# A hybrid transformer layer on one core: the SBUF tiles laid out anew, weight units at the top, streaming operands from the bottom up

## Chip, cores and metric

The kernel runs on one core of a Trainium2 chip. The metric is the device time of one execution in microseconds (us); lower is better. The on-chip memory SBUF has 128 partitions, and a tile occupies the same range of bytes in each of them; all sizes and places below are bytes of one partition. TensorE (PE in the profile) multiplies a stationary operand, which is loaded first (LDWEIGHTS, PEld in the profile), with a moving one that streams through. VectorE is DVE, ScalarE is ACT, GpSimd is POOL, and SP issues most of the DMAs.

## The reference

One layer over 1024 latent tokens of width 1024 with a context of 256 tokens. The input is normed and modulated, one combined projection feeds three token mixers, each mixer's output is lifted to the full width, gated and summed, and an output projection adds to the stream. Then a gated MLP with a depthwise convolution of width 3 follows, and a final norm.

```python
h = x * rsqrt(mean(x*x)) * gain * (1 + scale) + shift          # adaLN, also for the context
q, k, v (A), q, k, v (B), q, f, b, i, g (C), gates = split(h @ w_in)
yA = sliding_window_attention(A)        # 8 heads of 64, 2 kv heads, window 128, sink, context keys
yB = global_attention(B)                # q and k normed, axial rotary
yC = bidirectional_recurrence(C)        # 4 heads of 128
merged = sum(sigmoid(gate_n) * (y_n @ w_branch_n) for n in (A, B, C))
x = x + m2 * (merged @ w_out)
h = adaLN(x)
u = depthwise_conv3(h @ w_up)           # 2 x 2816 columns
x = x + m5 * ((u[:2816] * silu(u[2816:])) @ w_down)
out = rms_norm(x)
```

## The kernel before

Every float32 operand is split into two parts of 12 bits, a high one and the rest (hh and hl, yh and yl, h2h and h2l, ah and al, ph and pl, KH and KL, wh and wl), and each product is three matmuls in the type fp32r: wh with the high part, wh with the low part, wl with the high part (lines 158, 159 and 160 of `gemm_cm`). There the weights are stationary, 128x128, and the other operand streams, 512 columns in one matmul. `gemm_tm` (lines 168 to 170) has them the other way round: the activations are stationary, and 256 columns of weights stream. In the profile's names the streaming operand of a matmul stands first behind the arrow and the stationary one second.

A weight unit (`w_unit`) is loaded by SP into `wr` (three buffers of 4 KB), ScalarE casts it to `wh` and VectorE subtracts to get `wl`. These three tags lie in the pool `wp`, 36,864 bytes, open for the whole kernel.

The stages, in the order in which they run:

- modulation and norm of context and latent stream; context projections (czf, czb, czv, ckv); the layer input in two parts, hh and hl (32 KB each, pool `hp`, closed as `hpool` after the attention);
- branch C, the recurrence: its projections are zq, zf, zb, zv, zg, five groups of 192 matmuls that stream hh and hl; between them the scores on small tiles;
- projections of A and B by tokens (tm), results to DRAM; `gate_unit` (gz) computes gate values to DRAM, and many of its units are kept as filler for the attention;
- attention A, then B, one call of `attention` each with a pool of its own, `at0` and `at1`. A call first loads and casts K and V of all tokens (KH, KL, VHL) and then goes through 16 iterations, two for each block of 128 queries. `weave` runs three generators by turns: the scores of the next iteration (sbl and others, which stream KH and KL), the values of this one, and gate units. `values` transposes a block of probabilities (pp), ScalarE and VectorE split it into ph and pl (`PV_BUF` = 3 buffers each), and po, streaming ph and pl with VHL stationary, adds it up. At the end of an iteration yT goes to DRAM (`y_d`);
- merge (`merge_up`, pool `mp`): for each branch in the order C, A, B four tiles of y come back from DRAM (two buffers) and are split into yh and yl (six buffers each); br are the products with `w_branch`. The sums go into xm, in two parts into h2h and h2l (32 KB each);
- output projection (wo), streaming h2h and h2l, then the norm, which writes the layer's second input into the same h2h and h2l;
- FFN: 44 column tiles of w_up, each for two halves of 512 tokens (up, 24 matmuls for each half), whose results are convolved, gated and split into ah and al (five buffers each), and in seven groups w_down (dn, streaming ah and al; dl for the last group), summed into xm. Then the final norm and the store.

Pools are stacked from the two ends of a partition: `side="right"` stacks from the top (229,344) down, the default from the bottom up. The constants end at 19,584. A pool that closes leaves its bytes to the next one; with `reuse_waits="tile"` a new tile waits for the last readers of those old tiles that lay on its bytes. So the place of a tile sets whom its first writer waits for. Within an engine's queue the order is that of the program as the scheduler arranged it, and a waiting instruction holds back those behind it.

Of the kernel before, what the change touches and what calls it, by code (L numbers as in the profile page):

```python
# [10 lines left out]
F32R = mybir.dt.float32r  # L11
# [4 lines left out]
PSUM = bass.MemoryType.PSUM  # L16
DRAM = bass.MemoryType.DRAM

P = 128
D = 1024  # L20
# [24 lines left out]
# channel tiles whose shift and scale the vector engine sums, and the tiles after which they are finished  # L45
# [3 lines left out]
# tiles whose squares are summed by GpSimd before the final norm  # L49
# [11 lines left out]
# heads whose softmax sums are finished together  # L61
NB = 1

# channel-major column tiles of the packed input projection
# [7 lines left out]
def build(tc, ins, out, dbg=None):  # L72
    nc = tc.nc
    V, A, G, T, SP = nc.vector, nc.scalar, nc.gpsimd, nc.tensor, nc.sync
    with ExitStack() as top:
        const = top.enter_context(tc.tile_pool(name="const", bufs=1))
        wp = top.enter_context(tc.tile_pool(name="wp", bufs=3))
# [22 lines left out]
        # the table of the sigmoid is loaded while c is under way  # L100
# [33 lines left out]
        def w_unit(src, nk, ncol, lo_eng=None):  # L134
            """one weight unit [128, nk, ncol] -> (hi, lo) in 12-bit parts"""
            cnt[0] += 1
            n = nk * ncol
            with tc.high_priority(offset=wprio[0]):
                raw = wp.tile([P, 1024], F32, tag="wr", name=f"wr{cnt[0]}", bufs=WR)
                SP.dma_start(raw[:, :n], src)  # L140
                hi = wp.tile([P, 1024], F32R, tag="wh", name=f"wh{cnt[0]}", bufs=WH)
                lo = wp.tile([P, 1024], F32R, tag="wl", name=f"wl{cnt[0]}", bufs=WL)
                A.copy(hi[:, :n], raw[:, :n])  # L143
                (lo_eng or V).tensor_tensor(out=lo[:, :n], in0=raw[:, :n], in1=hi[:, :n].bitcast(F32),  # L144
                                            op=ALU.subtract)
            return (hi[:, :n].rearrange("p (k n) -> p k n", k=nk),
                    lo[:, :n].rearrange("p (k n) -> p k n", k=nk))

        def gemm_cm(psl, w, h, cols, k0=0, c0=0, nk=None, first=True, last=True, order=None):
            """psl[128 out, tokens] (+)= w[:, k, c0:c0+128]^T h[:, k0+k, cols]; three passes"""  # L150
            wh, wl = w
            hh, hl = h
            nk = nk or wh.shape[1]
            c = slice(c0, c0 + P)
            for n, k in enumerate(order or range(nk)):
                s = first and n == 0
                e = last and n == nk - 1
                T.matmul(psl, wh[:, k, c], hh[:, k0 + k, cols], start=s, stop=False)  # L158
                T.matmul(psl, wh[:, k, c], hl[:, k0 + k, cols], start=False, stop=False)  # L159
                T.matmul(psl, wl[:, k, c], hh[:, k0 + k, cols], start=False, stop=e)  # L160

        def gemm_tm(psl, ws, h, toks, k0=0, nk=KT):
            """psl[128 tokens, cols] = sum_k h[:, k, toks]^T w[k]"""
            hh, hl = h
            for k in range(nk):
                wh, wl = ws[k // 4]
                s, e = k == 0, k == nk - 1
                T.matmul(psl, hh[:, k, toks], wh[:, k % 4, :], start=s, stop=False)  # L168
                T.matmul(psl, hh[:, k, toks], wl[:, k % 4, :], start=False, stop=False)  # L169
                T.matmul(psl, hl[:, k, toks], wh[:, k % 4, :], start=False, stop=e)  # L170

# [1 line left out]
        def rms_row(pool, parts, n, name, tag="b", on_pe=False):  # L173
            """1/sqrt(sum/D + eps) of the tokens, on every partition: PSUM [128, n]; parts: squares to be summed"""
# [7 lines left out]
            if on_pe:  # L182
                # the parts are summed as they are transposed
# [26 lines left out]
        def finish_h(t, r, a, bi, ohh, ohl, x=None):  # L210
            """x * a * r + bi in two parts; t, or x where it is given, is the scratch for x * a * r"""
            V.scalar_tensor_tensor(out=t, in0=t if x is None else x, scalar=a, in1=r, op0=ALU.mult, op1=ALU.mult)
            A.activation(ohh, t, AF.Identity, bias=bi)
            V.scalar_tensor_tensor(out=ohl, in0=t, scalar=bi, in1=ohh.bitcast(F32), op0=ALU.add, op1=ALU.subtract)  # L214

        with ExitStack() as s0:
# [9 lines left out]
            # shift and scale of both streams, one channel tile after the other  # L226
# [6 lines left out]
            def mod_done(i, pm):  # L233
                """shift and scale of channel tile i, and the tile of h"""
# [67 lines left out]
            # lower bounds: softmax over the (length one) layer axis, cumulative sum minus the first  # L302
# [19 lines left out]
            def lat_norm():  # L322
                # squares summed on two engines: tiles 0-3 and 4-7
# [52 lines left out]
            def ctx_kv():  # L376
                # attention keys and values of the context
# [25 lines left out]
            # suffix (forward) and prefix (backward) decay products over the 256 context tokens  # L403
# [28 lines left out]
        def gate_unit(pool, n, i, mode):  # L432
            """gate pre-activations of branch n, channel tile i -> dram"""
# [22 lines left out]
        def mod_rest(pool):  # L456
            """modulation chunks 2..5 of the latent stream"""
# [37 lines left out]
        with ExitStack() as sp3:  # L495
# [3 lines left out]
            # tables [t, tt, (C|S), 64]: A as they are, B with the head-norm gains  # L499
# [52 lines left out]
        n0 = 10 + GATES_A  # L552
        for br, units in ((0, gates[10:n0]), (1, gates[n0:])):
            with ExitStack() as sa:
                ap_ = sa.enter_context(tc.tile_pool(name=f"at{br}", bufs=2, side="right", reuse_waits="tile"))
                nf = 16 * len(units)
                gen = gate_units(ap_, units, "b")
                attention(tc, nc, ap_, br, ins, kv_d[br], q_d[br], y_d, mm2, bank, ident, identr, gen, nf)
# [5 lines left out]
        fp = top.enter_context(tc.tile_pool(name="fp", bufs=1, side="right", reuse_waits="tile"))  # L564
        xm = fp.tile([P, KT, L], F32, tag="xm", name="xm")
        f2 = top.enter_context(tc.tile_pool(name="f2", bufs=1, side="right", reuse_waits="tile"))
# [5 lines left out]
        f3 = ExitStack()  # L572
        ff = f3.enter_context(tc.tile_pool(name="ff", bufs=2, reuse_waits="tile"))
# [3 lines left out]
        def sumsq(parts, src, i, name, n, NPOOL):  # L577
            """squares of tile i, summed over the tiles by two engines; the last one stays apart"""
# [10 lines left out]
        # x_mix = x + m2 * (merged @ w_out), its norm; by token halves  # L589
# [21 lines left out]
        def up(f):  # L611
# [19 lines left out]
            ah = ff.tile([P, 1, L], F32R, tag="ah", name=f"ah{f}", bufs=5)  # L631
            al = ff.tile([P, 1, L], F32R, tag="al", name=f"al{f}", bufs=5)
# [11 lines left out]
        for g, ng in enumerate(FFN_GROUPS):  # L644
# [3 lines left out]
            if g < NG - 1:  # L648
                for i in range(KT):
                    if g == NG - 2 and i == KT // 2:  # L650
                        # the last tile of the hidden layer, with sums still to run behind it
# [8 lines left out]
            else:  # L660
                # last group by blocks of tokens, each followed by the final norm
                o0 = 0
                # its weights: two units, four tiles of output channels in each
# [43 lines left out]
def forget(nc, pool, z, F, K, lb, oml, n, nm):  # L707
    """F = sigmoid(z) + lb sigmoid(-z); K = (1 - lb) sigmoid(-z)"""
# [7 lines left out]
def head_rms(nc, pool, z, nh, nm, mhalf):  # L716
    """[128, nh] of 1/sqrt(mean over 64 + eps)"""
# [10 lines left out]
def hgrn_head(nc, cp, h, H, ins, w_unit, gemm_cm, mm2, bank, ident, masks, lb, oml, st_ctx, gnc, mhalf, y_d):  # L728
# [23 lines left out]
    # QQ[:, 1]: forward, prefix products; QQ[:, 0]: backward, suffix products  # L752
# [3 lines left out]
    # values, token-major  # L756
# [14 lines left out]
    # scores S[j, t], one level of the binary tree at a time  # L771
# [39 lines left out]
    # chunk states  # L811
# [53 lines left out]
def weave(*gens):  # L865
    """emit generators side by side, each at an even pace: gens are (generator, number of steps)"""
# [13 lines left out]
def attention(tc, nc, ap_, br, ins, kv_d, q_d, y_d, mm2, bank, ident, identr, fill_gen, fill_steps):  # L880
# [19 lines left out]
    def prep(k0):  # L900
# [7 lines left out]
        for part, dst in ((0, KH), (1, KL)):  # L908
            if part == 0:
                kk = tl([P, 2, 2, 2, 64], "qs", f"kk{k0}{part}", dt=F32R)  # p, k, g, dup, e  # L910
# [15 lines left out]
    def qprep(it):  # L926
        """scaled queries of four heads, both parts stacked, transposed"""
# [22 lines left out]
    def values(it, PT, kts):  # L950
# [9 lines left out]
        for n, kt in enumerate(kts):  # L960
# [3 lines left out]
            ph = tl([P, 4, P], "ph", f"{it}{kt}", PV_BUF, F32R)  # L964
            pl = tl([P, 4, P], "pl", f"{it}{kt}", PV_BUF, F32R)
# [9 lines left out]
        # y^T of head pairs: rows 0-63 even head, 64-127 odd head  # L975
# [38 lines left out]
def softmax_window(nc, tl, mm2, tt, g, nm, QT, KH, KL, trir, identr, snk, nsnk, res):  # L1014
# [10 lines left out]
    for h in range(4):  # L1025
        # context keys in the second half of one bank, the window's in the next
# [10 lines left out]
        # -max(scores, sink)  # L1037
# [18 lines left out]
def softmax_global(nc, tl, mm2, g, nm, QT, KH, KL, res):  # L1056
    V, A, G, T = nc.vector, nc.scalar, nc.gpsimd, nc.tensor
    # negated maxima, sums: [:, 0, h] context part, [:, 1, h] latent part
# [14 lines left out]
    for h in range(4):  # L1073
# [10 lines left out]
        if h % NB == NB - 1:  # L1084
            # common maximum: factors exp(m_part - m) / sum
# [23 lines left out]
def merge_up(nc, mp, ins, gate_d, y_d, mg, mgh, mgl, w_unit, gemm_cm, mm2):  # L1109
    """merged = sum_n sigmoid(gate_n) * (y_n @ w_branch_n), split into two parts"""  # L1110
# [35 lines left out]
def _tile_w(w, nk, ncol):  # L1146
    """[nk*128, n*ncol] -> [n, 128, nk*ncol]"""
# [4 lines left out]
def prepare(inputs):  # L1152
# [15 lines left out]
    # head dimension: the even members of the rotated pairs first, then the odd ones  # L1168
# [24 lines left out]
    # constants of the shapes  # L1193
# [11 lines left out]
    cs = np.stack([np.cos(ang), np.sin(ang)], 1).astype(f)  # [1024, 2, 32]  # L1205
# [17 lines left out]
```

## Time and profile before

| what | value |
|---|---|
| median of 3 runs | 2263.78 us |
| lowest and highest | 2261.83 and 2265.91 us |
| profiled execution, its own time (span) | 2258.7 us |
| granted TensorE clock, mean | 0.993 |
| busy: PE, DVE, ACT, POOL | 96%, 61%, 39%, 12% |
| weight loads (PEld) | 80% |
| DMA | 180.33 MB, mean 80 GB/s |

The profile is of one execution on the chip; its span runs from the first to the last instruction. A row for a group of instructions gives line, engine, operation, tiles, shape and count, then the busy time and the mean duration of one, then the idle time of the engine before them and who ended it. A row of the timeline starts with the start (us) and the duration of one instruction. Matmuls are pipelined: one starts before the one before it has ended, so the durations in the rows (about 390 ns for 512 columns) are longer than the distances between starts.

### The profile page before, as it was taken

Reading aid. Unit: us, or ns where it says so; the run is one execution under the profiler, and the core shown is the slowest. Engines: PE = TensorE matmul, PEld = TensorE weight load, DVE = VectorE, ACT = ScalarE, POOL = GpSimd, SP = SyncE. Lnnn points to the kernel's source line nnn. Section 1 sums busy time; section 2 is a strip of 40 time slices with the busy share of each in tenths; the row PEclk is TensorE's granted clock in tenths of the full one; section 3 lists DMA queues with packets and bytes.
Section 4 is the critical chain, followed back from the end, with each engine's and each line's share of the span. In section 5 each row is a group of like instructions: output and inputs, shape, how many; then the busy total and the mean of one; then the engine's idle time right before and its main releaser. Section 6 shows DMA issues by size and latency. Waiting matters only on the chain. (4 is left out here: it accounts for less than half of the span.)

```text
span 2258.7 us, 29811 instructions
## 1 busy us (share of the span) xinstructions
PE 2176.2 (96%) x11400; PEld 1803.4 (80%) x11400; DVE 1380.8 (61%) x2458; ACT 884.7 (39%) x1614; POOL 272.0 (12%) x289
## 2 busy tenths in 40 slices
PE   7799999999999999999999999999999999999997
PEld 4778888889988888877777787778888878888886
DVE  6946666646566778699999757554434444444445
ACT  4522322321122777677777634333222122222223
POOL 1410000001022222133333100100000000000004
PEclk9999999999999999999999999999999999999998
DMA  7320110116643211211000453421120202111112
GB/s 310 119 67 29 47 38 29 52 66 197 201 156 123 78 57 50 87 34 33 31 29 27 160 180 132 142 90 38 38 66 28 69 18 70 31 57 55 33 51 76
DMA packets 80238, 180.33 MB, mean 80 GB/s; under 512 B 9056, under 2 KB 38112, under 8 KB 79072
## 3 DMA queue, kind: packets, MB, share of 16 engines
q1 hardware_dynamic: 79808, 178.37, 24.6%
q8 instruction: 90, 1.47, 0.3%
q14 instruction: 52, 0.43, 0.1%
q10 hardware_dynamic: 288, 0.07, 0.0%
HBM read 148.52 MB, written 29.88 MB: 79 GB/s over the span
## 5 line engine op out<-in xcount | busy, mean ns | idle before, releaser
L143 ACT CAST wh<-wr 128x1024 fp32r<-128x1024 f32 (+2 forms) x194 | 179.6, 927 | 724.4 <-PE up L159 301.8
L144 DVE TENSOR_TENSOR wl<-wr,wh 128x1024 fp32r<-128x1024 f32 (+2 forms) x189 | 206.4, 1093 | 378.6 <-ACT wh L143 366.4
L159 PE MATMUL up<-h2l,wh 128*128 128x512 f32 x704 | 279.2, 397 | 0.0
L158 PE MATMUL up<-h2h,wh 128*128 128x512 f32 x704 | 278.3, 396 | 0.0
L160 PE MATMUL up<-h2h,wl 128*128 128x512 f32 x704 | 276.4, 393 | 0.0
L968 DVE TENSOR_TENSOR pl<-pp,ph 128x512 fp32r<-128x512 f32 x236 | 159.0, 684 | 9.7 <-ACT ph L967 8.5
L158 PE MATMUL gz<-hh,wh 128*128 128x512 f32 x384 | 155.9, 406 | 3.5 <-ACT gs L448 3.4
L158 PEld LDWEIGHTS up<-h2h,wh 128*128 128x128 f32 x704 | 132.1, 188 | 32.8
L160 PEld LDWEIGHTS up<-h2h,wl 128*128 128x128 f32 x704 | 132.2, 188 | 32.5
L159 PEld LDWEIGHTS up<-h2l,wh 128*128 128x128 f32 x704 | 132.2, 188 | 31.0 <-DVE h2l L214 0.3
L967 ACT CAST ph<-pp 128x512 fp32r<-128x512 f32 x236 | 136.2, 585 | 44.4 <-PE pp L963 41.5
L160 PE MATMUL gz<-hh,wl 128*128 128x512 f32 x384 | 152.5, 397 | 0.0
L159 PE MATMUL gz<-hl,wh 128*128 128x512 f32 x384 | 152.0, 396 | 0.0
L158 PE MATMUL dn<-ah,wh 128*128 128x512 f32 x320 | 125.9, 393 | 0.4
L159 PE MATMUL dn<-al,wh 128*128 128x512 f32 x320 | 125.3, 392 | 0.0
L160 PE MATMUL dn<-ah,wl 128*128 128x512 f32 x320 | 125.0, 390 | 0.0
L658 DVE SCALAR_TENSOR_TENSOR xm<-dn,mods,xm 128x1024 f32<-128x1024 f32 x48 | 61.6, 1283 | 88.7 <-PE dn L160 88.1
L169 PE MATMUL tm<-wl,hh 128*128 128x256 f32 x384 | 108.9, 283 | 1.5 <-DVE wl L144 1.5
L168 PE MATMUL tm<-wh,hh 128*128 128x256 f32 x384 | 108.7, 283 | 0.0
L170 PE MATMUL tm<-wh,hl 128*128 128x256 f32 x384 | 108.7, 283 | 0.0
L957 PE MATMUL po<-ph,VHL 128*128 128x512 f32 x236 | 105.4, 446 | 1.3 <-ACT ph L967 1.3
L958 PE MATMUL po<-pl,VHL 128*128 128x512 f32 x236 | 99.4, 421 | 7.4 <-DVE pl L968 7.2
(833 smaller groups left out, 5101.8 us busy)
## 6 DMA issues: line engine op xcount, KB each, us to landing
wr<-in_w_cm SPq DMA_DIRECT2D x56, 512.0 KB, 3.8
wr<-in_w_up SPq DMA_DIRECT2D x44, 512.0 KB, 3.5
wmr<-in_w_mod SPq DMA_DIRECT2D x32, 512.0 KB, 4.5
gate_d<-gs SPq DMA_DIRECT2D x48, 256.0 KB, 2.3
sgt<-gate_d SPq DMA_DIRECT2D x24, 512.0 KB, 4.0
wm<-in_w_mod SPq DMA_DIRECT2D x8, 1024.0 KB, 14.3
wr<-in_w_tm SPq DMA_DIRECT2D x16, 512.0 KB, 3.7
wr<-in_w_out SPq DMA_DIRECT2D x16, 512.0 KB, 3.7
```

The costliest lines, as they stand in the source:

```text
L143: A.copy(hi[:, :n], raw[:, :n])
L144: (lo_eng or V).tensor_tensor(out=lo[:, :n], in0=raw[:, :n], in1=hi[:, :n].bitcast(F32), op=ALU.subtract)
L158: T.matmul(psl, wh[:, k, c], hh[:, k0 + k, cols], start=s, stop=False)
L159: T.matmul(psl, wh[:, k, c], hl[:, k0 + k, cols], start=False, stop=False)
L160: T.matmul(psl, wl[:, k, c], hh[:, k0 + k, cols], start=False, stop=e)
L168: T.matmul(psl, hh[:, k, toks], wh[:, k % 4, :], start=s, stop=False)
L169: T.matmul(psl, hh[:, k, toks], wl[:, k % 4, :], start=False, stop=False)
L170: T.matmul(psl, hl[:, k, toks], wh[:, k % 4, :], start=False, stop=e)
L957: T.matmul(po, vv, ph, start=n == 0, stop=False)
L958: T.matmul(po, vv, pl, start=False, stop=n == len(kts) - 1)
L967: A.copy(ph, pp)
L968: V.tensor_tensor(out=pl, in0=pp, in1=ph.bitcast(F32), op=ALU.subtract)
```

## The change

Every instruction computes what it did, and none is added or taken away. Tiles get other places. Comments and docstrings are removed as well; line numbers up to the attention stay the same and are one or two higher behind it.

```diff
-        wp = top.enter_context(tc.tile_pool(name="wp", bufs=3))
+        wp = top.enter_context(tc.tile_pool(name="wp", bufs=3, side="right"))
...
             with ExitStack() as sa:
-                ap_ = sa.enter_context(tc.tile_pool(name=f"at{br}", bufs=2, side="right", reuse_waits="tile"))
+                pv = sa.enter_context(tc.tile_pool(name=f"pv{br}", bufs=1, reuse_waits="tile"))
+                ap_ = sa.enter_context(tc.tile_pool(name=f"at{br}", bufs=2, reuse_waits="tile"))
...
-                attention(tc, nc, ap_, br, ins, kv_d[br], q_d[br], y_d, mm2, bank, ident, identr, gen, nf)
+                attention(tc, nc, ap_, pv, br, ins, kv_d[br], q_d[br], y_d, mm2, bank, ident, identr, gen, nf)
...
-        f2 = top.enter_context(tc.tile_pool(name="f2", bufs=1, side="right", reuse_waits="tile"))
+        f2 = top.enter_context(tc.tile_pool(name="f2", bufs=1, reuse_waits="tile"))
...
+        fa = f3.enter_context(tc.tile_pool(name="fa", bufs=5, reuse_waits="tile"))
         ff = f3.enter_context(tc.tile_pool(name="ff", bufs=2, reuse_waits="tile"))
...
-            ah = ff.tile([P, 1, L], F32R, tag="ah", name=f"ah{f}", bufs=5)
-            al = ff.tile([P, 1, L], F32R, tag="al", name=f"al{f}", bufs=5)
+            ah = fa.tile([P, 1, L], F32R, tag="ah", name=f"ah{f}")
+            al = fa.tile([P, 1, L], F32R, tag="al", name=f"al{f}")
```

In `attention`, the tiles ph and pl are taken from the new pool `pv`, with the same three buffers each.

Places that follow from the pools' order and the tile sizes (first byte, and the remainder of it by 128):

| tiles | stream in | before | rest | after | rest |
|---|---|---|---|---|---|
| wr, wh, wl | tm, ckv (stationary elsewhere) | 19,584 to 56,448 | 0 | 192,480 to 229,344 | 96 |
| hh, hl | z*, gz | 56,448 to 121,984 | 0 | 19,584 to 85,120 | 0 |
| KH, KL (second pass) | sbl | 122,592 to 143,072 | 96 | 97,408 to 117,888 | 0 |
| VHL (second pass) | (stationary) | 143,072 to 153,312 | 96 | 117,888 to 128,128 | 0 |
| ph, pl | po | 212,960 to 225,248 | 96 | 85,120 to 97,408 | 0 |
| yh, yl | br | 56,448 to 105,600 | 0 | 85,120 to 134,272 | 0 |
| h2h, h2l | wo, up | 131,040 to 196,576 | 96 | 19,584 to 85,120 | 0 |
| ah, al | dn, dl | 90,048 to 131,008 | 64 | 85,120 to 126,080 | 0 |
| xm | | 196,576 to 229,344 | 96 | 159,712 to 192,480 | 96 |

More of the change, by code (lines that the diff above doesn't have):

```diff
@@ L877, in weave, with attention @@
             gens.remove(e)
-def attention(tc, nc, ap_, br, ins, kv_d, q_d, y_d, mm2, bank, ident, identr, fill_gen, fill_steps):
+def attention(tc, nc, ap_, pv_pool, br, ins, kv_d, q_d, y_d, mm2, bank, ident, identr, fill_gen, fill_steps):
     V, A, G, T, SP = nc.vector, nc.scalar, nc.gpsimd, nc.tensor, nc.sync
@@ L963, in values @@
                 T.transpose(pp[:, h], PT(h, n), ident)
-            ph = tl([P, 4, P], "ph", f"{it}{kt}", PV_BUF, F32R)
-            pl = tl([P, 4, P], "pl", f"{it}{kt}", PV_BUF, F32R)
+            ph = pv_pool.tile([P, 4, P], F32R, tag="ph", name=f"ph{br}_{it}{kt}", bufs=PV_BUF)
+            pl = pv_pool.tile([P, 4, P], F32R, tag="pl", name=f"pl{br}_{it}{kt}", bufs=PV_BUF)
             with tc.high_priority(offset=V_PRIO):
```

## The prediction, made before the change was run

> **What bounds the kernel now.** I read the busy table, the chain of waits and the busy table by stretches first, to see which engine sets the end, and then, stage by stage, the starts of one matmul after another.
>
> ```profile
> PE 2176.2 (96%) x11400; PEld 1803.4 (80%) x11400; DVE 1380.8 (61%) x2458; ACT 884.7 (39%) x1614; POOL 272.0 (12%) x289
> ...
> PE 41%; DVE 2%; issue 1%; ACT 1%; POOL 1%; DMA 0%; DVEq 0%; SPq 0%; ACTq 0%; POOLq 0%
> ...
> 1660.00:2200.00 540.00, 539.70 (x2323) 435.56 (x2322) 225.73 (x205) 124.48 (x136) 0.00 (x0) 1.00 0.15 45
> ```
>
> TensorE (PE) is busy 96% of the span and is the only engine with weight in the chain. The last row is most of the FFN (window, length, then busy time and count on PE, weight loads, VectorE, ScalarE, GpSimd; then granted clock, DMA share): PE 539.70 of 540.00 us at clock 1.00, VectorE 225.73. Nothing waits there, so a stage ends sooner only if one matmul follows the other sooner. That pace is the quantity to read. The duration of a matmul row doesn't show it, since matmuls overlap; the distance of starts does. The next rows (matmuls of one line inside a stage: count, min/median/max ns, first and last start) come from undisturbed stretches, where each product is three matmuls, so one line starts once in three.
>
> ```profile
> L158 PE MATMUL zv<-hh,wh x16: 389/389/389, 156.2 to 166.4; 128*128 128x512 f32 x16
> ...
> L158 PE MATMUL br<-yh,wh x144: 389/389/395, 1305.7 to 1403.3; 128*128 128x512 f32 x144
> ...
> L159 PE MATMUL dn<-al,wh x16: 394/394/394, 1624.0 to 1634.3; 128*128 128x512 f32 x16
> ...
> L160 PE MATMUL wo<-h2h,wl x15: 394/394/394, 1439.7 to 1449.5; 128*128 128x512 f32 x15
> ...
> L158 PE MATMUL up<-h2h,wh x81: 394/394/394, 1534.4 to 1590.4; 128*128 128x512 f32 x81
> ```
>
> Distance per matmul: zv 10.2 us / 45 = 226.7 ns; br 97.6 / 429 = 227.5; dn 10.3 / 45 = 228.9; wo 9.8 / 42 = 233.3; up 56.0 / 240 = 233.3. All are 128x128 by 128x512 fp32r with the same three weight buffers and the same form of loop; zv and up even write the same PSUM tag. What differs is the place of the operand that streams (the first name behind the arrow). By the allocation order and tile sizes, in bytes of a partition: hh starts at 56,448 and yh at 56,448, both multiples of 128; ah and al lie behind the 704-byte cw, 64 past a multiple; h2h and h2l hang from the top, 229,344, 96 past a multiple. Height alone doesn't order them: ah and al (90,048 to 131,008) span the height of hl (89,216 to 121,984), and still dn is slower than zv. Alignment orders all five: 227, 229 and 233 ns for 0, 64 and 96 past a multiple.
>
> **The change part by part.** Nothing is added or taken away: the same instructions, DMAs and waits on data. Tiles move, and with them (a) the pace of matmuls and (b) who must wait for whose bytes. After it hh, yh, ah, h2h, ph and KH all start on multiples of 128, in the lower part; the weights hang from the top at 96 past a multiple.
>
> ```profile
> L159 PE MATMUL up<-h2l,wh 128*128 128x512 f32 x704 | 279.2, 397 | 0.0
> L159 PE MATMUL dn<-al,wh 128*128 128x512 f32 x320 | 125.3, 392 | 0.0
> ...
> L159 PE MATMUL wo<-h2l,wh 128*128 128x512 f32 x128 | 50.2, 393 | 0.0
> ...
> L957 PE MATMUL po<-ph,VHL 128*128 128x512 f32 x236 | 105.4, 446 | 1.3 <-ACT ph L967 1.3
> L1077 PE MATMUL sbl<-KH,QT 128*128 128x512 f32 x128 | 51.8, 404 | 0.0
> ```
>
> Times three lines (two for po and sbl) these are the counts.
> 1. up: 2112 matmuls from 233.3 to 226.7 ns, 2112 x 6.67 = -14.1 us. Bounds: 0 (the pace doesn't follow) and -14.1.
> 2. wo: 384 x 6.67 = -2.6.
> 3. dn: 960 from 228.9 to 226.7, 960 x 2.2 = -2.1. Its place is aligned but not lower than before; if height were the cause, 0.
> 4. Attention: 472 po and 256 sbl stream ph, pl, KH, KL, now 96 past a multiple. At 6.5 ns that would be -4.7, but they alternate with other work, and there the aligned gz runs no faster:
>
> ```profile
> 959.97 0.39 PE L160 MATMUL gz<-hh,wl 128*128 128x512 f32 x1
> 960.20 0.39 PE L158 MATMUL gz<-hh,wh 128*128 128x512 f32 x1
> 960.43 0.40 PE L1077 MATMUL sbl<-KH,QT 128*128 128x512 f32 x1
> ...
> 962.30 0.39 PE L159 MATMUL gz<-hl,wh 128*128 128x512 f32 x1
> ```
>
> gz, gz, sbl are 230 ns apart, and the eight sbl take 1.87 / 8 = 234. I take a third, -1.5; ends 0 and -4.7.
>
> 5. The weights' new place. No 512-column matmul of before has a stationary operand off the 128 grid beside an aligned streaming one, so I bound it by 256-column ones. In ckv the stationary chh hangs from the top (96 past); in tm both operands are aligned:
>
> ```profile
> 100.92 0.28 PE L168 MATMUL ckv<-wh,chh 128*128 128x256 f32 x1
> ...
> 107.68 0.28 PE L168 MATMUL ckv<-wh,chh 128*128 128x256 f32 x1
> ...
> 563.87 0.28 PE L168 MATMUL tm<-wh,hh 128*128 128x256 f32 x1
> ...
> 565.67 0.28 PE L168 MATMUL tm<-wh,hh 128*128 128x256 f32 x1
> L158 PEld LDWEIGHTS up<-h2h,wh 128*128 128x128 f32 x704 | 132.1, 188 | 32.8
> L957 PEld LDWEIGHTS po<-ph,VHL 128*128 128x128 f32 x236 | 44.6, 189 | 6.2 <-ACT ph L967 2.8
> ```
>
> ckv: 6.76 us over 57 matmuls, 118.6 ns; tm: 1.80 over 15, 120.0. The misplaced stationary operand costs nothing, and its weight load (VHL, also 96 past) takes 189 ns beside 188. I take 0. Upper end: the whole misalignment, 6.67 ns, on each matmul that streams an aligned tile (rival C). tm streams the weights, 96 past in future; ckv, its like, streams aligned ones, so no row of that kind shows the price: 0, and at most 1152 x 6.67 = 7.7.
>
> 6. Attention to merge. Before, the merge pool lies on hh and hl, which are free when the last gate unit ends. So y is cast, and merge matmuls run, between the last values:
>
> ```profile
> 1264.00:1277.00 13.00, 12.67 (x66) 9.51 (x66) 10.05 (x13) 10.74 (x15) 0.00 (x0) 1.00 0.76 262
> ...
> 1262.58 1.05 ACT L1120 CAST yh<-y 128x1024 fp32r<-128x1024 f32 x1
> ...
> 1264.11 1.22 DVE L1121 TENSOR_TENSOR yl<-y,yh 128x1024 fp32r<-128x1024 f32 x1
> ...
> 1264.41 0.39 PE L158 MATMUL br<-yh,wh 128*128 128x512 f32 x1
> ...
> 1273.48 1.08 ACT L1120 CAST yh<-y 128x1024 fp32r<-128x1024 f32 x1
> ...
> 1276.27 1.05 ACT L1120 CAST yh<-y 128x1024 fp32r<-128x1024 f32 x1 [0.97 <-DMA y<-y_d]
> ...
> 1276.67 0.40 PE L958 MATMUL po<-pl,VHL 128*128 128x512 f32 x1
> ```
>
> From the first br to the last po start 22 br matmuls, 22 x 0.227 = 5.0 us of PE work in the gaps of the values. After, the first yh slots (85,120 on) lie on ph and pl (85,120 to 97,408) and yl slots on KL and VHL, all in use until the last po. So the first cast waits for that po; behind it on ScalarE and VectorE stand only the same tail's ytmp and yT and the next casts, and PE waits for the cast. The tail alone needs between 12.67 - 5.0 = 7.7 us and its old 12.7; then 1.05 us of cast, then the 5.0. Loss between 7.7 + 1.05 + 5.0 - 12.7 = 1.1 and 6.1; I take 3.5, the middle, since nothing shows how the tail runs by itself. Later casts keep their distance, 1276.27 - 1273.48 = 2.8 us (two y buffers, refilled from DRAM as before); the 24 matmuls (5.4 us) that the first two y tiles allow cover that.
>
> 7. Costed at nothing: the start of the second attention pass, whose K and V tiles lay in part on those of the first pass already and now lie on them fully; its loads were issued when the first pass ended (row below), hidden by gate matmuls (PE busy 309.71 of 329.00 us over the pass, row below); without that cover, the 19.3 us idle of that row would grow by the 3.0 us from the load's issue to the first cast. And cw and xr, now behind yl's last slots until the last br matmul (start 1403.8): they were issued 5 us later than that anyway.
>
> ```profile
> 935.00:1264.00 329.00, 309.71 (x1731) 247.45 (x1730) 286.88 (x684) 245.64 (x582) 101.83 (x128) 1.00 0.13 41
> ...
> 935.46 0.97 SPq L902 DMA_DIRECT2D qf_kv<-kv_d  x2
> ...
> 938.45 0.41 ACT L906 CAST VHL<-qf_kv 128x256 fp32r<-128x256 f32 x1 [0.19 <-DMA qf_kv<-kv_d]
> ...
> 1408.64 0.38 SPq L575 DMA_DIRECT2D cw<-in_conv  x1
> 1409.07 1.37 SPq L598 DMA_DIRECT2D xr<-in_xT  x3
> ```
>
> Sum: -14.1 - 2.6 - 2.1 - 1.5 + 3.5 = -16.8 us. The profiled execution's own time is its span, 2258.7 us; that becomes 2241.9. The median of the runs shown is 2263.78, 5.1 above it; the same difference gives 2247.0. A change under 0.2% (4.5 us) can't be told from none here.
>
> [...]
>
> **The rivals.**
> B. The pace belongs to the stage, not to the place (the engines that read its PSUM tiles, or the weights' stream). Then only term 6 is left: 2263.78 + 3.5 = 2267.3, within 0.2%. For it: up, wo and dn are later stages with other consumers. Against it: wo and up have different consumers and the same 233.3, and br, between them and zv, has 227.
> C. The change makes it slower: misalignment of either operand costs the 6.67 ns once per matmul, and now every weight is misaligned. Place: all stages that ran at 227 to 229. up and wo stay at 233.3 (no gain); zq to zg (960) and br (576) lose 6.67 each, 10.2; some 480 undisturbed gz 3.2; dn 960 x 4.4 = 4.2; with term 6 +21.1: 2284.9. It decides from 16.8 us / 6144 matmuls with weights = 2.7 ns each. For it: no 512-column row excludes it. Against it: ckv and the 189 ns load; and sbl, with both operands 96 past, has 234 and not 240, though that is what "once" would give too.
> D. The handover eats the gain: the tail and the casts run strictly one after another, and y loads queue on SP behind the last yT store, so that PE idles for each of the first four y tiles (3 x 2.8 us, the spacing of casts, on top of 3.5): 2247.0 + 8.4 = 2255.4. Against it: loads of the first two y tiles are free of the tail's bytes.
>
> **How the numbers follow.** A, the working above: 0.78, its own range 2241 to 2253 (from term 4 at -4.7 with term 6 at 1.1, to terms 3 and 4 at 0 with term 6 at 6.1). B 0.08, C 0.08, D 0.06. Predicted 2247.0. The range 2238 to 2263 holds A and D and leaves out B and C. Faster by over 0.2% (under 2259.3): A and D, 0.84 (D at 2255.4 is below the bound; a dearer one would be a tie); same B, 0.08; slower C, 0.08.
>
> **What would show it.** Up and wo: 80 triples of up in 54.4 us instead of 56.0, the row's three lines 680 ns apart. dn 226.7 (alignment) or 228.9 (height). zv and br unchanged at 227: if they rise to 233, C. The first yh cast starts after the last po of the second pass and PE's idle time there is one to six us. The prediction is wrong if up stays at 233.3, or if zv, gz and br slow down.

## The result, and the profile after

The changed kernel is slower: 2288.78 us median (2287.48 to 2290.11, 4 runs) against 2264.77 us for the kernel before in the same comparison; the ratio is 1.0111, 95% interval 1.0099 to 1.0123. The profiled spans are 2285.7 and 2258.7 us, so 27.0 us are to be found in the traces; that is 3 us more than the medians differ by, since the traced execution of the kernel before was a quick one.

The busy table of the page and one stretch of the FFN look as before:

```profile
PE 2198.9 (96%) x11400; PEld 1807.5 (79%) x11400; DVE 1381.6 (60%) x2458; ACT 886.2 (39%) x1614; POOL 271.9 (12%) x289
...
1680.00:2220.00 540.00, 540.00 (x2302) 433.07 (x2302) 226.29 (x205) 122.93 (x134) 0.00 (x0) 1.00 0.15 45
```

TensorE is as full as it was; only the count tells that 540 us held 2323 matmuls before and 2302 now. The next view is the matmuls of one line in undisturbed stretches, the same rows as before (count, min/median/max ns, first and last start):

```profile
L158 PE MATMUL zv<-hh,wh x16: 392/397/400, 156.6 to 167.1; 128*128 128x512 f32 x16
...
L160 PE MATMUL br<-yh,wl x136: 392/397/400, 1329.9 to 1424.8; 128*128 128x512 f32 x136
...
L159 PE MATMUL dn<-al,wh x16: 392/397/400, 1645.2 to 1655.7; 128*128 128x512 f32 x16
...
L159 PE MATMUL wo<-h2l,wh x15: 392/397/400, 1459.7 to 1469.6; 128*128 128x512 f32 x15
...
L158 PE MATMUL up<-h2h,wh x79: 392/397/400, 1559.9 to 1614.7; 128*128 128x512 f32 x79
```

zv takes 10.5 us / 45 = 233 ns, br 94.9 / 405 = 234.3, dn 10.5 / 45 = 233, wo 9.9 / 42 = 236, up 54.8 / 234 = 234.2. From the single starts in the trace all five settle at 234.3. So none of the five became faster: zv, br and dn, which ran at 227 or 229, now run at the same pace as up and wo, and those two are themselves 1 ns slower than before. The durations show it too: zv had 389/389/389.

The last view is the place between the second attention pass and the merge: the timelines of TensorE, SP (start, duration, and the idle time before it in brackets) and ScalarE, and the busy table by stretches, whose third number from the end is the granted clock:

```profile
1277.84 0.49 PE L960 MATMUL po<-pl,VHL 128*128 128x512 f32 x1 [0.18 <-DVE pl L970]
1285.75 1.22 PE L158 MATMUL br<-yh,wh 128*128 128x512 f32 x2 [7.42 <-ACT yh L1122]
...
1270.00 10.40 SPq L986 DMA_DIRECT2D y_d<-yT  x2
1280.53 0.88 SPq L1121 DMA_DIRECT2D y<-y_d  x2
...
1284.66 1.04 ACT L1122 CAST yh<-y 128x1024 fp32r<-128x1024 f32 x1 [5.54 <-DMA y<-y_d]
...
1276.00:1285.00 9.00, 2.12 (x9) 1.02 (x7) 2.23 (x4) 1.81 (x5) 0.00 (x0) 0.71 0.44 126
1285.00:1290.00 5.00, 4.21 (x8) 2.40 (x9) 2.45 (x2) 3.96 (x4) 0.00 (x0) 0.50 0.87 324
```

After the last po TensorE stands for 7.42 us and then works at half clock (0.50 granted from 1285 to 1290 us). The cast that it waits for was itself waiting for the load of y, not for ph and pl: ScalarE was free 5.54 us earlier. And that load was issued late, since it stood on SP behind the store of the last yT (the row of 10.40 us holds two stores, the second one waiting for its data).

Distances between first and last starts give the sum by stages, in us against before:

| stretch | before | after | difference |
|---|---|---|---|
| start to the last gz | 1258.6 | 1264.5 | +5.9 |
| last gz to the last br | 145.2 | 161.0 | +15.8 |
| last br to the last wo | 94.0 | 92.7 | -1.3 |
| last wo to the last dl | 747.8 | 754.6 | +6.8 |

The rest, -0.3, lies behind the last dl. Of the +5.9, 4.2 us arise between the first zq and the last zg, where 960 matmuls at 7.6 ns would be 7.3, so part of the slower pace does not show in the time there. Of the 15.8, 576 br at 7.6 ns are 4.4; the handover, what the passage from the attention to the merge costs beyond that, is 11.4. In the last row 960 dn at 5.4 ns are 5.2 and 2112 up at 1.0 ns 2.0.

### The profile page after: what moved, and what is told of

Read it like the earlier page. It is cut to its first block, busy times and chain, and to the rows that moved or that the text cites. A ratio compares the mean times of both kernels' runs of the same rounds, so it can differ in the third digit from the quotient of the medians.

```text
span 2285.7 us, 29802 instructions
## 1 busy us (share of the span) xinstructions
PE 2198.9 (96%) x11400; PEld 1807.5 (79%) x11400; DVE 1381.6 (60%) x2458; ACT 886.2 (39%) x1614; POOL 271.9 (12%) x289
## 5 line engine op out<-in xcount | busy, mean ns | idle before, releaser
L160 PE MATMUL gz<-hh,wl 128*128 128x512 f32 x384 | 152.9, 398 | 0.0
```

## The experiments

The shorthands: "grid" is the theory of the prediction (each operand by itself should start on a multiple of 128 bytes), which the result left standing in the form of rival C; "difference", which comes up on the way, is the theory that the pace goes by the stationary start less the streaming start; "height" says that weights high up or streaming tiles high up are slow.

**All tiles on multiples of 128, heights as before (all_aligned).** knb and qnb (512 bytes) go from the constants to the pool of hh to make room, here and in every other layer kernel below except f2_low.

```diff
+        padr = top.enter_context(tc.tile_pool(name="padr", bufs=1, side="right"))
+        pad_r = padr.tile([P, 24], F32, tag="padr", name="padr")
...
         cw = ff.tile([P, 2 * FT, 4], F32, tag="cw", name="cw", bufs=1)
+        pad_f = ff.tile([P, 16], F32, tag="padf", name="padf", bufs=1)
```

> The layout of before, with 96 bytes left free at the top of SBUF and 64 behind cw, so that every tile that a matmul reads (also h2h, h2l, ah, al, KH, KL, VHL, ph, pl) starts on a multiple of 128 bytes; heights and neighbours stay, the weights stay at the bottom. Grid theory (the pace of a 512-column matmul is set by the remainder by 128 of either operand's start): up and wo go from 233.3 to 226.7 ns, dn from 228.9 to 226.7, zv and br stay at 227; -14.1 - 2.6 - 2.1, and 0 to -4.7 in the attention, no loss at the handover: 2240 to 2246 us. Height theory (what matters is that the streaming tiles lie low, or the weights lie high): up stays at 233.3, 2264 us. Theory that the pace belongs to the stage: 2264 us.

Measured: 2248.53 us, ratio 0.9941 (0.9924 to 0.9959).

```profile
L160 PE MATMUL up<-h2h,wh x77: 389/389/389, 1554.9 to 1606.6; 128*128 128x512 f32 x77
...
L161 PE MATMUL dn<-al,wh x61: 392/398/398, 1609.6 to 1651.6; 128*128 128x512 f32 x61
```

up takes 51.7 / 228 = 226.8 ns at its old height, so height is out for the streaming side. But dn does not follow. It settles at 233.0 by the single starts, slower than the 228.9 of before, although ah and al now are on the grid. That is a miss of the grid theory, and the time lies 2.5 us above its range.

**The changed kernel with the weights on a multiple of 128 (top_aligned).** The same 96 bytes at the top of the changed kernel.

> The changed kernel with 96 bytes left free at the top, so that the weights start on a multiple of 128 too; everything stays as high as in the changed kernel. Grid theory: zv, br, dn, wo, up all at 226.7 ns; the handover to the merge keeps its loss of some 12 us; before - 18.8 - 1.5 + 12, about 2256 us. Height theory (weights at the top are slow to load): all stay at 234.3, as the changed kernel, 2289 us.

Measured: 2254.46 us, ratio 0.9966 (0.9952 to 0.9980).

```profile
L160 PE MATMUL zv<-hh,wh x16: 389/389/389, 156.0 to 166.2; 128*128 128x512 f32 x16
...
L161 PE MATMUL up<-h2l,wh x82: 389/389/389, 1554.7 to 1609.8; 128*128 128x512 f32 x82
```

Weights at the top load as well as at the bottom: up 55.1 / 243 = 226.7. 96 bytes are worth 34 us of the changed kernel's time, and the height of the weights is out. The grid theory's 2256 us fits, but it is no evidence against a rule by the distance of the two operands: here every pair of the five stages is a multiple of 256 apart as well.

**The layout of before with the weights alone off the grid (weights_off).**

```diff
+        pada = top.enter_context(tc.tile_pool(name="pada", bufs=1))
+        pad_a = pada.tile([P, 24], F32, tag="pada", name="pada")
         wp = top.enter_context(tc.tile_pool(name="wp", bufs=3))
+        padb = top.enter_context(tc.tile_pool(name="padb", bufs=1))
+        pad_b = padb.tile([P, 8], F32, tag="padb", name="padb")
```

> The layout of before, with the weights alone 96 past a multiple of 128, still at the bottom; all other tiles keep their remainders. Grid theory: zv, gz, br and dn rise to 234.3 ns, up and wo by 1 at most: 960 x 7.6 + 576 x 7.6 + half or all of 1152 x 7.6 + 960 x 5.4 + 2496 x 1.0 = 24 to 28 us where they run undisturbed, so about 2283 to 2291 us. Height theory: 2264 us, paces as before. The handover is that of before in both.

Measured: 2258.70 us, ratio 0.9976 (0.9966 to 0.9986): a little faster where 20 us and more were expected.

```profile
L162 PE MATMUL zv<-hh,wh x16: 393/395/397, 159.4 to 169.9; 128*128 128x512 f32 x16
...
L162 PE MATMUL up<-h2h,wh x81: 389/389/389, 1554.9 to 1609.3; 128*128 128x512 f32 x81
```

zv rose, to 233.3 (234.3 was expected), but up fell to 54.4 / 240 = 226.7, with both of its operands 96 past a multiple. The grid theory falls here: what counts is not where each operand lies.

**Pairs of places by themselves (pairs).** One `seg` per pair, no other engine at work:

```python
def seg(name, m, mo, s, so, n=512, cnt=48):
    p = ps.tile([P, 512], F32, tag="p", name=name)
    for j in range(cnt):
        k = j % KS
        T.matmul(p[:, :n], s[:, so // 4 + k * 128:so // 4 + (k + 1) * 128],
                 m[:, mo // 4 + k * 512:mo // 4 + k * 512 + n], start=j == 0, stop=j == cnt - 1)
```

> The layer is left out, zeros are written: segments of 48 matmuls 128x128 by 128x512 fp32r, one for each pair of places of the streaming and the stationary operand (0, 32, 64, 96 past a multiple of 128, then 4, 8, 16 and 48 for one of them), the same high up in SBUF, and 256-column ones. Nothing else runs. Grid theory: 226.7 ns for 0 and 0, about 229 where one is 64 past, 233 to 234 where either is 96 or 32 past, once and not twice where both are; the same high up; 120 ns for all 256-column pairs. Height theory: high segments slower than low ones at the same remainders. If contention with other engines makes the difference, all segments have one pace.

Two letters give the two remainders (a 0, b 32, c 64, d 96; the streaming one first):

```profile
L49 PE MATMUL paa<-mov,sta x48: 390/393/404, 34.9 to 45.8; 128*128 128x512 f32 x48
...
L49 PE MATMUL pbb<-mov,sta x48: 390/393/404, 90.7 to 101.6; 128*128 128x512 f32 x48
...
L49 PE MATMUL pac<-mov,sta x48: 388/392/398, 57.3 to 68.0; 128*128 128x512 f32 x48
```

paa has both on the grid and is slow: from the starts of 24 matmuls in its middle 232.3 ns. paa, pbb, pcc and pdd agree within 0.7 ns, paa and pbb down to min, median and max; pac and pbd have 228.9; pba, pcb and pdc 234.2 to 234.5. So the pace goes by the difference of the two starts, and with no other engine at work contention with one is not what makes it. And 0 at 226.7 in the layer stands against 0 at 232.3 here: in the layer zv's stationary start less its streaming start is -24,576, a multiple of 256; here it was 16,512, 128 over one. Hence the difference theory: the pace is a function of (stationary start - streaming start) by 256. A few bytes can count as well: a streaming start at 4 (a difference of 124) gave 240.0, a stationary one at 4 (132) 226.7. High up in SBUF the like pairs have 232.7 and 233.3 (tdd, taa) beside paa's 232.3, so height gives 1 ns at most. The 256-column segments have 117.8 to 120.0.

**That theory on the layer, twice (weights_128, all_256).** The first puts 32 fp32 words before and behind `wp` in place of the 24 and 8 above, so that only the distance of the weights changes, by 128. The second makes pad_f of all_aligned 48 words instead of 16.

> The layout of before with the weights alone put 128 bytes further from the other tiles: every tile keeps its remainder by 128 (weights 0, hh and yh 0, ah 64, h2h 96). Grid theory (each operand by itself on a multiple of 128): nothing changes, 2264 us. Difference theory (the pace is a function of the stationary start less the streaming start, by 256): z, gz and br go from a difference of 0 to 128, 226.7 to 232.4 ns; dn from 192 to 64, 228.9 to 233.3; up and wo from 160 to 32, 233.3 both: 960 x 5.7 + 576 x 5.7 + half or all of 1152 x 5.7 + 960 x 4.4 = 16 to 20 us slower, 2279 to 2283 us.

> The kernel with all tiles on multiples of 128 (all_aligned), with ah and al put 128 bytes higher. There dn has a difference of 128 to its weights, now 0 by 256. Grid theory: ah and al stay on a multiple of 128, dn keeps 233.0 ns, 2248 us. Difference theory: dn goes to 226.7, 960 x 6.3 = 6.0 us less, 2242 us; up, wo, z and br stay at 226.7 in both.

Measured: weights_128 2272.66 us, ratio 1.0039 (1.0025 to 1.0052); all_256 2244.15 us, ratio 0.9913 (0.9900 to 0.9926), the fastest kernel of the study.

```profile
L162 PE MATMUL zv<-hh,wh x16: 390/393/404, 158.2 to 168.7; 128*128 128x512 f32 x16
...
L162 PE MATMUL dn<-ah,wh x45: 392/393/398, 1620.8 to 1651.6; 128*128 128x512 f32 x45
```

```profile
L160 PE MATMUL dn<-ah,wh x62: 389/389/389, 1609.8 to 1651.3; 128*128 128x512 f32 x62
```

In weights_128 (first fence) zv settles at 232.4 and dn at 233.3, each as expected to 0.1 ns; even the 390/393/404 of the isolated pairs at this difference comes back. The time rose by less than expected, 11.5 us of span and 8.4 by the medians: the gz units between attention work, which I had counted in part or in full, don't pay (the first to the last po take 518.7 us against 518.4), and z, br and dn alone are 5.5 + 3.3 + 4.1 = 12.9. In all_256 dn has the 226.7 of the rest.

**The differences alone (pairs_diff).**

> The layer is left out, zeros are written: segments of 64 matmuls 128x128 by 128x512 fp32r, the stationary start less the streaming start in steps of 32 bytes over 512, then 4, 8, 16, 124, 132, 248, 252; then two segments in which both starts alternate, so that a matmul's own pair is 0 apart and the next weights, loaded while it streams, are 96 and -96 off, and the reverse. Difference theory: the same pace at d and d + 256; 0 has 226.7, 96 has 234.3, 128 has 232.4, 192 has 228.9, the others about 233.3 ns. If the weights loaded meanwhile are what counts, the first alternating segment has 234 and the second 226.7; if a matmul's own pair counts, the reverse. Grid theory: 0 at 226.7 and every 128 the same.

```profile
L44 PE MATMUL da<-mov,sta x64: 389/389/397, 31.5 to 45.8; 128*128 128x512 f32 x64
...
L44 PE MATMUL dd<-mov,sta x64: 391/397/400, 75.9 to 90.6; 128*128 128x512 f32 x64
...
L44 PE MATMUL di<-mov,sta x64: 389/389/397, 150.2 to 164.5; 128*128 128x512 f32 x64
...
L44 PE MATMUL dl<-mov,sta x64: 391/397/400, 194.6 to 209.4; 128*128 128x512 f32 x64
...
L44 PE MATMUL xo<-mov,sta x64: 391/395/401, 372.4 to 387.1; 128*128 128x512 f32 x64
L44 PE MATMUL xn<-mov,sta x64: 387/395/397, 387.3 to 401.8; 128*128 128x512 f32 x64
```

da and di (256 apart) are alike, and so are dd and dl; all eight pairs of segments agree within 0.1 ns. The paces over 40 matmuls in the middle of a segment, beside the undisturbed matmuls of the layer kernels:

| difference by 256 | alone, ns | in the layer, ns |
|---|---|---|
| 0 | 226.7 | before zv 226.7, br 226.7; all_256 dn 226.7; f2_low, weights_off up 226.7 |
| 32 | 233.3 | weights_128 up 233.3 |
| 64 | 233.3 | weights_128 dn 233.3 |
| 96 | 234.3 | after zv, br, dn, wo, up 234.3 |
| 128 | 232.4 | all_aligned dn 233.0; weights_128 zv 232.4 |
| 160 | 233.3 | before up and wo 233.3; weights_off dn 233.3 |
| 192 | 228.9 | before dn 228.9 |
| 224 | 233.3 | weights_off zv 233.3 |

The alternating segments are half a hit. With a matmul's own pair 0 apart and the next weights off, the pace is 234.0, so the own pair is not what alone counts; but with own pairs off and the next 0 apart it is 230.0 and not 226.7. No segment alternates the starts with all differences 0, so what the alternation itself costs is not known, and whether the weights loaded meanwhile make the loss is not shown. In steps of 4 bytes the difference is not the whole rule: 124 had 240.0 when the streaming start was moved and 231.7 when the stationary one was; 132 and 252, off every step of 32, are as fast as 0 (226.7).

**Only h2h and h2l moved to the bottom (f2_low).** One word, `side="right"`, taken from the pool `f2` of before; the merge pool then lies on tiles of the second attention pass.

> Of the change only h2h and h2l moved to the bottom (onto hh and hl); the merge pool then comes to lie on KH, KL and VHL of the second attention pass. Weights at the bottom, ph and pl at the top as before. Difference theory: up and wo fall from a difference of 160 to 0, 233.3 to 226.7 ns, -16.7 us; br stays at 226.7 and dn at 228.9. Handover theory (the merge pool on tiles of the attention makes y wait and puts its loads behind the last yT): PE idle and cold between the last po and the first br as in the changed kernel, +12 us; together about 2259 us. Without a handover cost: 2247 us.

Measured: 2258.91 us, ratio 0.9979 (0.9969 to 0.9988).

```profile
1268.61 10.41 SPq L984 DMA_DIRECT2D y_d<-yT  x2
1279.15 0.88 SPq L1119 DMA_DIRECT2D y<-y_d  x2
...
1283.96 1.22 PE L158 MATMUL br<-yh,wh 128*128 128x512 f32 x2 [7.00 <-ACT yh L1120]
```

The handover appears by itself, with the same order on SP and 7.00 us of idle TensorE. Last gz to last br takes 157.0 us against 145.2, so +11.8; the last two stretches are 2.5 and 13.9 us shorter, near the -16.7 that terms 1 and 2 of the prediction name. The stretch up to the last gz is 4.5 us longer in this trace, though no tile used before the merge was moved; 2.6 of that are there at the first gz already. So that row of a single trace is good to a few us only, in the table of the changed kernel too; the distance from the first zq to the last zg, 324.9 us here and 325.2 before, is steadier.

**The merge's loads off SP (top_aligned_yq, then top_aligned_ysq).** Both are top_aligned with issuing engines changed:

```diff
-            SP.dma_start(y, y_d[n, k])
+            (G if j == 0 else SP).dma_start(y, y_d[n, k])
...
-                SP.dma_start(s, gate_d[n, i])
+                (G if j == 0 and i < 2 else SP).dma_start(s, gate_d[n, i])
```

The first has only the upper edit.

> The kernel with the weights at the top and all differences 0 by 256 (top_aligned, 2254.5 us), with one line of the merge changed: the four y loads of its first branch are issued by GpSimd instead of SP, where they stood behind the store of the last yT. If that order is what makes the handover dear: the first two y tiles are in SBUF before the last po, the first cast starts within 1 us of it, PE idles 1 to 2.5 us instead of some 7.5, its clock stays at full speed, and 7 to 9 us come back: 2246 to 2248 us. If the cast's wait for ph and pl by itself, or the room of the y tiles, is the cost: 2252 to 2255 us.

> The kernel before this one (top_aligned_yq) had its y tiles in time, but ScalarE's queue held a sigmoid on the first gate tile ahead of the first y cast, and that tile's load stood on SP behind the last yT store (cast at 1279.58 us, 7 us after the last po). Here the first two gate tiles are loaded by GpSimd's queue too. If the order on SP is the cost: the casts follow the last ytmp directly (1273 to 1274 us), PE idles 1 to 2.5 us, 6 to 8 us less than top_aligned: 2246 to 2248 us. If yet another wait takes its place, or the loads from GpSimd's queue cost as much: 2253 to 2257 us.

Measured: 2257.19 us, ratio 0.9979 (0.9968 to 0.9991), for the first, no gain; 2250.31 us, ratio 0.9942 (0.9926 to 0.9959), for the second.

```profile
1272.81 0.36 ACT L984 COPY ytmp<-po 64x256 f32<-64x256 f32 x1
1273.19 1.28 ACT L1137 ACT_TABLE_LOAD   x1
1278.62 1.06 ACT L1137 ACTIVATE sgt<-sgt 128x1024 f32<-128x1024 f32 x1 [4.14 <-DMA sgt<-gate_d]
1279.58 1.98 ACT L1124 CAST yh<-y 128x1024 fp32r<-128x1024 f32 x2
```

```profile
1273.77 0.36 ACT L984 COPY ytmp<-po 64x256 f32<-64x256 f32 x1
1274.16 2.00 ACT L1124 CAST yh<-y 128x1024 fp32r<-128x1024 f32 x2
...
1275.26 0.73 PE L160 MATMUL br<-yh,wh 128*128 128x512 f32 x2 [1.90 <-ACT yh L1124]
...
1275.00:1280.00 5.00, 4.22 (x11) 3.11 (x12) 2.38 (x3) 4.44 (x5) 1.06 (x2) 0.66 0.47 138
1280.00:1282.00 2.00, 0.86 (x4) 0.30 (x2) 0.47 (x1) 1.04 (x1) 0.00 (x0) 1.00 0.77 240
1282.00:1287.00 5.00, 4.47 (x13) 3.24 (x12) 1.98 (x2) 1.91 (x2) 0.00 (x0) 0.66 0.51 179
```

In the first kernel (first fence) y was there, but ScalarE had the sigmoid of a gate tile ahead of the casts, and that tile's load stood behind the same yT store: a new wait took the old one's place. In the second the casts follow ytmp directly and TensorE idles 1.90 us. Last gz to last br goes from 157.7 (top_aligned) to 152.9 us: 4.8 of 12.5 us came back (4.2 by the medians), not 6 to 8. The order on SP is shown as a cause for that part alone. In the 7.7 us that are left the clock still falls (0.66 in two of the last three rows) and later y tiles still come one by one (TensorE idles 1.14 us again before 1281.55); what each of these costs was not separated.

**The shape (pairs_shape).**

> The layer is left out, zeros are written: segments of 64 matmuls at a difference of 0, 96 and 128 (by 256), with 512, 448, 384, 320 and 256 streaming columns, then with 64 and 32 stationary columns in place of 128. If the load of the next weights and the stream meet in SBUF: fewer stationary columns lose less than 128 do (7.6 ns at 96, 5.7 at 128), and the loss shows at every number of streaming columns of 320 and more. If the loss is a fixed cost of the pair of addresses, it is the same for 32 columns.

With 512 columns the three differences give 226.7, 234.4 and 232.5 ns; with 448 columns 202.7, 200.0 and 204.0; with 384, 173.3, 173.3 and 175.6; with 320, 146.7 each. The loss at 96 is gone below 512 columns. With 256 columns it is 120.0, 118.7 and 118.7. With 64 stationary columns the paces are 230.0, 231.4 and 229.3, with 32 they are 231.7, 230.7 and 230.7: 96 and 128 lose less than with 128 columns, as the first expectation had it, but 0 loses too, and the first expectation's loss at 320 columns and more isn't there. So neither expectation holds as it stood, and why 512 columns are special stays open.

## Why the prediction was wrong

- The likeliest case failed at its step 5, "the weights' new place: I take 0". The weights were not a bystander: the pace goes by the distance between both operands, and moving hh, yh, ah, h2h and the weights all at once put the pairs of all five stages 96 apart by 256, the slowest of the eight steps. They run at 234.3 ns where 226.7 was forecast. Undone by 96 bytes, the changed kernel gains 34 us (top_aligned).
- The reading that led there, "alignment orders all five", fitted before because all weights of before had one place by 256. A remainder of the streaming tile and a distance to the weights could not be told apart in its rows: 0, 64 and 96 past a multiple were differences of 0, 192 and 160. Only two of eight steps are fast (226.7 ns at 0 and 228.9 at 192, the others 232.4 to 234.3), and one of them was taken for the rule.
- The bound by ckv, tm and the 188 ns load was of the wrong kind: 256-column matmuls lose nothing at any of the five differences tried (0, 32, 96, 128 and 224; 120.0 ns or less in every such segment), and the duration of a weight load doesn't show the pace (188 ns in up and in zv, before and after).
- Terms 1 to 3 had the right size for a layout with a difference of 0: predicted -18.8 together, and the last two stretches of top_aligned are 2.8 and 15.7 us shorter, 18.5. In after they came out as -1.3 and +6.8.
- Term 4, -1.5 in the attention, was near nothing: in all_256 the stretch from the first to the last po is 518.0 us against 518.4. There was nothing to gain by the difference: ph (212,960) and VHL (143,072) lie a multiple of 256 apart before and after the change, and so do KH and QT. That both operands of a pair were 96 past a multiple made the pair look misplaced.
- Term 6 was mis-sized: 3.5 taken, at most 6.1 allowed, 11.4 measured. Its place was right. Its cause was incomplete: in the changed kernel the first cast waited for the load of y behind the last yT store on SP, an order that rival D had named, and not for ph and pl. With the y and gate loads off SP 4.8 of top_aligned's 12.5 us came back; how the other 7.7 divide between the tail by itself, the lower clock and the later y loads stays open. D's sum of 11.9 came near by luck: it counted three waits of 2.8 us, and the trace has one of 7.42, two short ones (0.94 and 0.52 us) and a clock of 0.50 from 1285 to 1290 us.
- Rival C came within 4 us (2284.9 against 2288.78) with a wrong mechanism and a chance of 0.08. That was luck in the number: the loss is no price of one misplaced operand, as weights_off shows, where up has both operands 96 past a multiple and 226.7 ns. Its observation that sbl has 234 with both operands off, which it says "once" would give too, was no evidence, since the pair of sbl is 0 apart by 256; in such short series between other work even a difference of 0 doesn't settle at 226.7 (the eight sbl take 1.87 us).
- What makes the loss is not shown here. In xo, with its own pairs 0 apart and only the next weights off, the pace is 234.0 instead of 226.7 ns, but what its alternation costs by itself is not known.

## What to carry to other kernels

A pace of matmuls that differs between stages of one shape is worth a look at addresses, of both operands: for fp32r matmuls of 128x128 by 128x512, put stationary and streaming tiles a multiple of 256 bytes apart (here -20 us for 0.3 KB of padding, all_256) and confirm it by the distance of starts, not by durations. Other shapes have to be measured; at 448 columns the order was another (200.0 ns at 96, 202.7 at 0). Before moving a tile, write down every pair that it is in; a property that only one side was seen to vary in is not that side's property. And a pool laid on tiles that are in use late can delay more than its first writer: here its loads came to stand behind the late stores of their queue (the y load at 1280.53 us behind the two yT stores' 10.40 us, with TensorE idle for 7.42), and so did other loads that share it (the gate loads at 1281.74).

## What the runs showed that I had not expected

- The pace of 128x512 fp32r matmuls depends on the distance of the operands in steps far below a tile: 226.7 ns at 0, 228.9 at 192, 232.4 to 234.3 at the other multiples of 32 by 256, and 240.0 in one of two pairs 124 apart. At 448 columns 96 is even faster than 0 (200.0 against 202.7 ns).
- The clock fell without a long idle stretch too. In the changed kernel it was 0.50 over 5 us (1285 to 1290) behind a gap of 7.42 us, but in top_aligned_ysq the longest gap of TensorE in the handover was 1.90 us, and the granted clock was 1.00 from 1273 to 1275 us, 0.66 over the next 5 us, then 1.00, then 0.66 again over 5 us. The first fall followed gaps of 1.90 and 0.53 us, the second one gaps of 1.14 and 0.53 us, each time with TensorE waiting for the parts of y that ScalarE and VectorE make.
